# Large SBUF tiles on multiples of 512 bytes, and two query blocks in one visit of the attention

## The chip, the cores and the metric

One core of a Trainium2 chip runs the whole layer. The metric is the device time of one execution in microseconds (us); three runs of the kernel before gave 609.85, 610.11 and 610.28, median 610.11. Engines are called as in the profile: PE (matrix engine), PEld (its weight loads), DVE (vector), ACT (scalar), POOL (GpSimd), SP (sync, which issues most DMAs).

## The reference

The kernel computes one decoder layer for 512 tokens of width 1024 in float32. Cut to what matters:

```python
h = x @ w_in                                     # 1024 -> 9 x 1024
ua, va, za, qh, kh, vh, zb, ga, gb = split(h)
va = layer_norm(gelu(va)); sa = einsum(tril(w_s), va) + b_s
ya = gelu(ua) * sa * silu(za)
q, k = rope(qh) * 64 ** -0.5, rope(kh)           # 8 heads, two maps of 64 each
for each block of 128 queries:                   # causal
    sc = q_block @ k.T                           # two maps per head
    pr = softmax(where(kpos <= qpos, sc, -inf))
    o = (pr[map 0] - lam * pr[map 1]) @ v        # 128 values per head
yb = rms_norm(o) * 0.8 * silu(zb)
merged = sigmoid(ga) * (ya @ w_a) + sigmoid(gb) * (yb @ w_b)
ple = sigmoid(x @ w_pg) * (p @ w_ple)
out = layer_norm(2 ** 0.25 * x + merged @ w_out + ple)
```

## The kernel before

Every large product is done in three passes on numbers cut in two: a high part (rounded for the fast single-pass mode of PE) and a low part (the rest). `three` issues high x high, high x low and low x high, so a product costs three matmuls of 128 x 128 stationary by 512 moving columns; line 268, in `product`, issues all of them. The large products by token blocks use seven sub-products instead of eight (`quad`). The weights come as units of 128 x 1024 floats (512 KB) by DMA into `wr` tiles; ACT makes the high part (`wh`, line 389), DVE subtracts it (`wl`, line 392). Units are asked for, cut and used in a fixed rotation: `next_unit` works two to three units ahead.

The order of everything else is set by a clock that counts matmuls of the main stream: `product` adds one, and then runs what has come due in `agenda`, a heap of functions which `later(n, fn)` puts n matmuls ahead. All instructions are issued in that one order, and the engines' queues keep it (`manual_schedule`). So "23 later" below means 23 matmuls of the main stream.

The attention is woven into the stretch that projects keys, queries and ua (`rope`, `ua_pair`) and za. For each of 8 heads there are 4 blocks of 128 queries; block i has (i + 1) x 128 keys. `scores` (line 769) multiplies q with two forms of k into two `sc` banks (one per map); DVE adds the mask, scales and takes the minimum (line 776), then ACT takes the exponential with its row sum (line 782). `combine` weighs the two maps on DVE; `transposes` turns the result through PE with the identity `ident` into the one `tr` bank, which ACT copies out (line 805); `values` (line 814) multiplies by v into the head's `po` bank. `PERIOD` gives the distance of the blocks of a head in matmuls, 13, 16, 20 and 23 (72 per head; in the last two heads times 0.78), `COMBINE` when the maps are combined after the scores. The transposes of a block come with the scores of the block after next, the values with those of the one after that: at one point in the main stream PE does values of one block, transposes of another and scores of a third. This is called a visit here. After the last block, `squares`, `norm`, `scale`, `gated` and `turned` normalize the head and turn it (`TAIL`, `LAST_TAIL`).

The tiles of SBUF come from pools that are packed one after another: `consts`, `wraw`, `wsp`, `big` and `attn` (later `post`) from the left, `turning` (later `late`) from the right. Every tile is rounded to 32 bytes. `consts` holds the identity, some constants and rings of small tiles (`small`, one ring per tag).

Of the kernel before, what the change touches and what calls it, by code (L numbers as in the profile page):

```python
# [13 lines left out]
F32 = mybir.dt.float32  # L14
# [3 lines left out]
AF = mybir.ActivationFunctionType  # L18
# [3 lines left out]
P = 128  # L22
# [27 lines left out]
PERIOD = (13, 16, 20, 23)  # L50
COMBINE = (10, 11, 13, 12)
LAST_TURNS = (14, 27, 45)
PAIR = 144
TAIL = (2, 14, 26, 44, 56)
LAST_TAIL = (2, 10, 20, 32, 42)
# [178 lines left out]
def hybrid_layer(ctx: ExitStack, tc: tile.TileContext, a, out: bass.AP):  # L234
# [4 lines left out]
    consts = ctx.enter_context(tc.tile_pool(name="consts", bufs=1))  # L239
    wraw = ctx.enter_context(tc.tile_pool(name="wraw", bufs=1))  # L240
# [237 lines left out]
    ident = consts.tile([P, P], F32, name="ident")  # L478
# [10 lines left out]
    mhalf = consts.tile([P, 8], F32, name="mhalf")  # L489
# [17 lines left out]
    def small(shape, name, bufs=6):  # L507
        return consts.tile(shape, F32, name=name, tag=name, bufs=bufs)
# [254 lines left out]
    def scores(h, i):  # L763
        n = (i + 1) * P
        q, k0, k1 = stacks["q", h], stacks["k", h], stacks["kx", h]
        sc = [pbank("sc", 2) for _ in range(2)]
        for m in range(2):
            for o, kk in enumerate((k0, k1)):
                pe.matmul(sc[m][:, :n], q[:, m, i * P:(i + 1) * P], kk[:, m, :n],  # L769
                          start=o == 0, stop=o == 1)  # L770
        pr = [ap_.tile([P, T], F32, name=f"p{m}", tag=f"p{m}", bufs=3) for m in range(2)]
        if i == 0:
            todo["st", h] = small([P, NT, 4], "sth", 2)
        st = todo["st", h][:, i, :]
        for m in range(2):
            dve.tensor_tensor_reduce(out=pr[m][:, :n], in0=sc[m][:, :n], in1=mask[:, T - n:],  # L776
                                     scale=-(DK ** -0.5), scalar=3e38, op0=OP.add, op1=OP.min,
                                     accum_out=st[:, m:m + 1])
            if m == 0:
                dve.tensor_scalar(out=st[:, 0:1], in0=st[:, 0:1], scalar1=-math.log(T),  # L780
                                  scalar2=None, op0=OP.add)
            act.activation(pr[m][:, :n], pr[m][:, :n], AF.Exp, bias=st[:, m:m + 1], scale=-1.0,  # L782
                           accum_out=st[:, 2 + m:3 + m])
        todo[h, i] = pr, st

    def combine(h, i):
        n = (i + 1) * P
        pr, st = todo[h, i]
        r1 = small([P, 1], "r1")
        dve.reciprocal(out=r1, in_=st[:, 3:4])  # L790
        rho = small([P, 1], "rho")
        dve.tensor_scalar(out=rho, in0=r1, scalar1=st[:, 2:3], scalar2=neglam[:, 0:1],
                          op0=OP.mult, op1=OP.mult)
        dve.scalar_tensor_tensor(out=pr[0][:, :n], in0=pr[1][:, :n], scalar=rho[:, 0:1],
                                 in1=pr[0][:, :n], op0=OP.mult, op1=OP.add)
        todo[h, i] = pr[0]

    def transposes(h, i):
        n = (i + 1) * P
        ad = todo[h, i]  # L800
        tr = pbank("tr", 1)
        for j in range(i + 1):
            pe.transpose(tr[:, j * P:(j + 1) * P], ad[:, j * P:(j + 1) * P], ident)  # L803
        at = ap_.tile([P, T], F32, name="at", tag="at", bufs=2)
        act.activation(at[:, :n], tr[:, :n], AF.Copy)  # L805
        todo[h, i] = at

    def values(h, i):
        at = todo.pop((h, i))
        if i == 0:  # L810
            todo["po", h] = pbank("po", 1)
        po = todo["po", h]
        for j in range(i + 1):
            pe.matmul(po[:, i * P:(i + 1) * P], at[:, j * P:(j + 1) * P],  # L814
                      v[:, j, h * P:(h + 1) * P], start=j == 0, stop=j == i)

# [43 lines left out]
    def block(h, i, starts):  # L860
        e = NT * h + i
        later(starts[e], scores, h, i)
        later(starts[e] + COMBINE[i], combine, h, i)
        later(starts[e + 2], transposes, h, i)
        later(starts[e + 3], values, h, i)
        if i == NT - 1:
            tail = TAIL if h < 5 else LAST_TAIL
            for d, fn in zip(tail, (squares, norm, scale, gated)):
                later(starts[e + 3] + d, fn, h)

    def attention():
        starts = []
        for h in range(NH):
            stretch = 1.0 if h < NH - 2 else STRETCH
            at = PAIR * (h // 2) + BEGIN + h % 2 * sum(PERIOD) * stretch
            for n in PERIOD:
                starts.append(round(at))
                at += n * stretch
        starts += [starts[-1] + n for n in LAST_TURNS]
        for h in range(NH):  # L880
            for i in range(NT):
                block(h, i, starts)
        for h in range(NH - 1):
            later(starts[NT * h + 9], turned, h)
        later(starts[-1] + LAST_TAIL[4], turned, NH - 1)

# [214 lines left out]
    def rstd_of(st):  # L1101
        mv = small([P, 2], "mv")
        dve.bn_aggr(out=mv, in_=st)
        dve.tensor_scalar(out=mv[:, 1:2], in0=mv[:, 1:2], scalar1=EPS, scalar2=None, op0=OP.add)
        rs = small([P, 1], "rs")
# [343 lines left out]
```

## Time and profile before

| | us |
|---|---|
| median of 3 runs | 610.11 |
| profiled execution | 610.13 |
| its span (first to last instruction) | 608.2 |
| PE busy / DVE busy / ACT busy / POOL busy | 600.1 / 464.8 / 346.7 / 125.4 |
| idle of PE at the start, after the last matmul | 1.3, 6.7 |
| mean granted clock of PE over the span | 0.997 |

"Busy" counts the time in which at least one instruction of the engine runs. The matmuls are pipelined: one of 512 columns is shown some 0.39 us long, and the next starts before it ends, so the pace is read from starts, not from lengths. An instruction's row has its line, engine, operation, output and inputs by the names of the tiles, and the shape. In the groups, after the bar, stand busy us and mean ns, then the idle time before the group and what ended it.

### The profile page before, as it was taken

How to read it: one execution, taken by the hardware profiler on the slowest of the kernel's cores; microseconds unless marked ns; L12 is line 12 of the kernel's file. 1: busy time of each engine (PE TensorE's matmuls, PEld its weight loads, DVE VectorE, ACT ScalarE, POOL GpSimd, SP SyncE). 2: the span in 40 equal slices, each digit the busy share in tenths (PEclk: the TensorE clock that was granted, in tenths of full speed). 3: DMA queues.
4: the chain of work that ended last, by engine and by line, in shares of the span. 5: the costliest groups of instructions: out<-in, count | busy, mean ns of one | idle time of the engine just before them, and what ended most of it. 6: DMA issues, size and time to landing. Idle time of an engine off the chain costs nothing.

```text
span 608.2 us, 8270 instructions
## 1 busy us (share of the span) xinstructions
PE 600.1 (99%) x2880; PEld 503.1 (83%) x2880; DVE 464.8 (76%) x770; ACT 346.7 (57%) x537; POOL 125.4 (21%) x133
## 2 busy tenths in 40 slices
PE   9999999999999999999999999999999999999995
PEld 6888888888888888888888888888888888888885
DVE  6995645588789789678965788779687887879476
ACT  6656475755745745746676666554776565555310
POOL 1234121041252432422110321331120011110011
PEclk9999999999999999999999999999999999999998
DMA  8689899697887896892579988976999578997002
GB/s 309 228 246 182 252 205 227 237 240 252 277 208 277 273 258 230 240 313 61 150 310 288 305 241 217 273 175 191 286 244 306 172 206 250 253 256 288 27 35 103
DMA packets 44541, 138.23 MB, mean 227 GB/s; under 512 B 5940, under 2 KB 7092, under 8 KB 44148
## 3 DMA queue, kind: packets, MB, share of 16 engines
q1 hardware_dynamic: 34436, 102.97, 46.8%
q0 software_dynamic: 9488, 34.35, 30.6%
q8 instruction: 22, 0.36, 0.2%
q10 hardware_dynamic: 576, 0.39, 0.2%
q14 instruction: 19, 0.16, 0.1%
HBM read 118.69 MB, written 29.49 MB: 244 GB/s over the span
## 4 chain that ended last, share of the span: by engine, by line
PE 98%; DVE 1%; DMA 0%; DVEq 0%; issue 0%
PE ps_pp L268 56%; PE ps_sc L268 22%; PE ps_tx L268 9%; PE ps_sc L769 3%; PE ps_po L814 3%; PE ps_tr L803 1%; PE ps_po L268 1%; PE ps_tr L268 1%; PE ps_tr L1133 1%; PE ps_po L1133 1%; PE ps_tx L857 1%; DMA xr<-in_xT 0%; PE ps_po L1319 0%; PE ps_tr L1319 0%; DVE base L1361 0%; DVE xl L295 0%
## 5 line engine op out<-in xcount | busy, mean ns | idle before, releaser
L392 DVE TENSOR_TENSOR wl<-wr,wh 128x1024 fp32r<-128x1024 f32 x133 | 165.4, 1250 | 36.7 <-ACT wh L389 36.5
L389 ACT ACTIVATE wh<-wr 128x1024 fp32r<-128x1024 f32 x133 | 139.4, 1054 | 68.7 <-PE ps_pp L268 20.5
L268 PE MATMUL ps_pp<-xh,wh 128*128 128x512 f32 x232 | 91.2, 394 | 0.0
L268 PE MATMUL ps_pp<-xh,wl 128*128 128x512 f32 x232 | 91.0, 393 | 0.0
L268 PE MATMUL ps_pp<-xl,wh 128*128 128x512 f32 x232 | 90.4, 391 | 0.1
L365 POOL DMA_DIRECT2D wr<-in_w x30 | 25.8, 872 | 153.6 <-DVE wl L392 150.6
L268 PE MATMUL ps_pp<-wl,xh 128*128 128x512 f32 (+1 forms) x148 | 56.9, 384 | 0.0
L268 PE MATMUL ps_pp<-wh,xl 128*128 128x512 f32 (+1 forms) x148 | 56.8, 384 | 0.0
L268 PE MATMUL ps_pp<-wh,xh 128*128 128x512 f32 (+1 forms) x148 | 56.7, 383 | 0.0
L782 ACT ACTIVATE p<-p,sth 128x128 f32<-128x128 f32 (+3 forms) x64 | 35.5, 556 | 28.2 <-DVE sth L780 28.0
L268 PEld LDWEIGHTS ps_pp<-xl,wh 128*128 128x128 f32 x232 | 43.6, 188 | 9.3 <-DVE xl L295 0.5
L268 PEld LDWEIGHTS ps_pp<-xh,wh 128*128 128x128 f32 x232 | 43.5, 188 | 9.0 <-ACT wh L294 0.6
L268 PEld LDWEIGHTS ps_pp<-xh,wl 128*128 128x128 f32 x232 | 43.6, 188 | 8.7
L776 DVE CUSTOM_DVE_ANT_0 p<-ps_sc,mask 128x128 f32<-128x128 f32 (+3 forms) x64 | 31.0, 484 | 19.3 <-PE ps_sc L769 19.1
L268 PE MATMUL ps_sc<-wl,xsh 128*128 128x512 f32 x88 | 34.5, 392 | 0.0
L268 PE MATMUL ps_sc<-wh,xsh 128*128 128x512 f32 x88 | 34.4, 390 | 0.0
L268 PE MATMUL ps_sc<-wh,xsl 128*128 128x512 f32 x88 | 34.3, 390 | 0.0
L805 ACT ACTIVATE at<-ps_tr 128x128 f32<-128x128 f32 (+3 forms) x32 | 13.9, 436 | 32.9 <-PE ps_tr L803 27.5
L715 POOL TENSOR_TENSOR hl<-m,hl 128x512 fp32r<-128x512 f32 x16 | 23.4, 1502 | 43.9 <-ACT hl L710 26.6
L268 PEld LDWEIGHTS ps_pp<-wl,xh 128*128 128x128 f32 x148 | 27.8, 188 | 5.4
L268 PEld LDWEIGHTS ps_pp<-wh,xh 128*128 128x128 f32 x148 | 27.8, 188 | 5.4
L268 PEld LDWEIGHTS ps_pp<-wh,xl 128*128 128x128 f32 x148 | 27.8, 188 | 5.4
(304 smaller groups left out, 1335.2 us busy)
## 6 DMA issues: line engine op xcount, KB each, us to landing
wr<-in_w SPq DMA_DIRECT2D x83, 512.0 KB, 5.2
wr<-in_w POOLq DMA_DIRECT2D x30, 512.0 KB, 6.7
wa<-in_w POOLq DMA_DIRECT2D x12, 512.0 KB, 6.2
k<-hl SPq DMA_DIRECT2D x16, 256.0 KB, 4.8
q<-hl SPq DMA_DIRECT2D x16, 256.0 KB, 3.9
ws_va<-in_w POOLq DMA_DIRECT2D x8, 512.0 KB, 9.8
wr<-ws_va SPq DMA_DIRECT2D x8, 512.0 KB, 4.7
kx<-hl SPq DMA_DIRECT2D x12, 256.0 KB, 4.5
```

Of the source, the lines that this page charges most:

```text
L268: pe.matmul(ps, s, m, start=start, stop=stop, skip_group_check=read_within)
L365: pool.dma_start(out=raw[u], in_=weights(STEPS[FOLLOWS[u]][1]), accum_op=OP.add)
L389: act.activation(h, raw[u], AF.Copy)
L392: dve.tensor_tensor(out=l, in0=raw[u], in1=h.bitcast(F32), op=OP.subtract)
L715: pool.tensor_tensor(out=hl[:, 3 - j, :], in0=m[2 * j], in1=hl[:, j, :].bitcast(F32), op=OP.subtract)
L769: pe.matmul(sc[m][:, :n], q[:, m, i * P:(i + 1) * P], kk[:, m, :n], start=o == 0, stop=o == 1)
L776: dve.tensor_tensor_reduce(out=pr[m][:, :n], in0=sc[m][:, :n], in1=mask[:, T - n:], scale=-(DK ** -0.5), scalar=3e38, op0=OP.add, op1=OP.m ...
L782: act.activation(pr[m][:, :n], pr[m][:, :n], AF.Exp, bias=st[:, m:m + 1], scale=-1.0, accum_out=st[:, 2 + m:3 + m])
L803: pe.transpose(tr[:, j * P:(j + 1) * P], ad[:, j * P:(j + 1) * P], ident)
L805: act.activation(at[:, :n], tr[:, :n], AF.Copy)
L814: pe.matmul(po[:, i * P:(i + 1) * P], at[:, j * P:(j + 1) * P], v[:, j, h * P:(h + 1) * P], start=j == 0, stop=j == i)
L1133: pe.matmul(sa[:, t * P:(t + 1) * P], va[:, t, g * P:(g + 1) * P], aux[0][:, 0, g, :], start=True, stop=True)
```

## The change

Two things are changed.

First, the addresses. The identity moves from `consts` to a pool of its own (`edge`) at the right end of SBUF, in a tile of 248 columns of which 128 are used; `mhalf` grows from 8 to 80 columns; `mv` and `rs` take their tiles from the rings `r1` and `rho` that the attention has used. With that, `wr`, `wh`, `wl`, `xh`, `xl`, the tiles of the attention and those of the right side begin at multiples of 512 bytes. Before, those on the left began 96 bytes, those on the right 480 bytes past such a multiple. The free 384 bytes between the two sides are used up.

Second, the attention. Blocks 0 and 1 of a head become one group: in one `sc` bank per map block 0 has columns 0 to 127 and block 1 columns 128 to 383. Scores, combine, transposes (one copy out) and values of both are issued together, instruction for instruction as before. The periods become 24, 23 and 25 (72 again), the combine 15, 13 and 12, the tail shorter. The new `GROUPS` lists groups, blocks and columns.

PE, head 1 (values and transposes beside its first scores are still those of head 0). The numbers tell buffers apart, so equal numbers are one tile. `k` and `kx` are the two forms of the keys, `ps_sc` the two score banks, `ps_pp` a bank of the main stream. Before, the visit with the scores of block 0:

```order
L814 MATMUL ps_po_1219<-v_124,at_1224 128x128 x2
L803 MATMUL ps_tr_1290<-ident_98,p0_1167 128x128 x3
L769 MATMUL ps_sc_1296<-k_494,q_669 128x128
L769 MATMUL ps_sc_1296<-kx_1006,q_669 128x128
L769 MATMUL ps_sc_1297<-k_494,q_669 128x128
L769 MATMUL ps_sc_1297<-kx_1006,q_669 128x128
L268 MATMUL ps_pp_1181<-xh_91,wl_1053 128x512
```

and, 13 matmuls of the main stream later, that with the scores of block 1:

```order
L814 MATMUL ps_po_1219<-v_124,at_1294 128x128 x3
L803 MATMUL ps_tr_1341<-ident_98,p0_1232 128x128 x4
L769 MATMUL ps_sc_1348<-k_494,q_669 128x256
L769 MATMUL ps_sc_1348<-kx_1006,q_669 128x256
L769 MATMUL ps_sc_1349<-k_494,q_669 128x256
L769 MATMUL ps_sc_1349<-kx_1006,q_669 128x256
L268 MATMUL ps_pp_1328<-xh_91,wh_1109 128x512
```

Now one visit has the scores of both blocks:

```order
L820 MATMUL ps_po_1282<-v_127,at_1209 128x128 x3
L807 MATMUL ps_tr_1286<-ident_101,p0_1150 128x128 x3
L775 MATMUL ps_sc_1292<-k_497,q_672 128x128
L775 MATMUL ps_sc_1292<-kx_1009,q_672 128x128
L775 MATMUL ps_sc_1293<-k_497,q_672 128x128
L775 MATMUL ps_sc_1293<-kx_1009,q_672 128x128
L775 MATMUL ps_sc_1292<-k_497,q_672 128x256
L775 MATMUL ps_sc_1292<-kx_1009,q_672 128x256
L775 MATMUL ps_sc_1293<-k_497,q_672 128x256
L775 MATMUL ps_sc_1293<-kx_1009,q_672 128x256
L270 MATMUL ps_pp_1176<-xh_94,wl_1056 128x512
```

The eight score matmuls stand together; the values and transposes beside them are those of other groups. One visit of four per head is gone.

DVE, a later head: the rows that read the scores (`ISA` is the masked minimum, with its accumulator) and what stands behind them. Before, block 0 alone, with the subtraction for a weight unit (line 392) and the combine of block 0 (790, 792) behind it:

```order
L776 ISA p0_1540,sth_1542<-ps_sc_1534,mask_110 128x128
L776 ISA sth_1542 128x1
L780 TENSOR_SCALAR sth_1542<-sth_1542 128x1
L776 ISA p1_1541,sth_1542<-ps_sc_1535,mask_110 128x128
L776 ISA sth_1542 128x1
L392 TENSOR_TENSOR wl_1502<-wr2_1311,wh_1501 128x1024
L851 TENSOR_TENSOR on_1417<-on_1417,yb_754 128x512
L790 RECIPROCAL r1_1563<-sth_1542 128x1
L792 TENSOR_SCALAR rho_1565<-r1_1563,sth_1542,neglam_196 128x1
L794 SCALAR_TENSOR_TENSOR p0_1540<-p1_1541,rho_1565,p0_1540 128x128
```

Now, both blocks (the lines are shifted by 4):

```order
L780 ISA p0_1777,sth_1779<-ps_sc_1775,mask_113 128x128
L780 ISA sth_1779 128x1
L784 TENSOR_SCALAR sth_1779<-sth_1779 128x1
L780 ISA p1_1778,sth_1779<-ps_sc_1776,mask_113 128x128
L780 ISA sth_1779 128x1
L780 ISA p0_1777,sth_1779<-ps_sc_1775,mask_113 128x256
L780 ISA sth_1779 128x1
L784 TENSOR_SCALAR sth_1779<-sth_1779 128x1
L780 ISA p1_1778,sth_1779<-ps_sc_1776,mask_113 128x256
L780 ISA sth_1779 128x1
L394 TENSOR_TENSOR wl_1718<-wr2_1547,wh_1717 128x1024
```

Four reads of the score banks stand in one piece where there were two and two; line 394, the old 392, comes behind all of them.

The diff:

```diff
--- before.py
+++ after.py
@@ -47,12 +47,13 @@
 SWAP = 290
 BEGIN = 14
 STRETCH = 0.78
-PERIOD = (13, 16, 20, 23)
-COMBINE = (10, 11, 13, 12)
+GROUPS = (((0, slice(0, 128)), (1, slice(128, 384))), ((2, slice(0, 384)),), ((3, slice(0, 512)),))
+PERIOD = (24, 23, 25)
+COMBINE = (15, 13, 12)
 LAST_TURNS = (14, 27, 45)
 PAIR = 144
-TAIL = (2, 14, 26, 44, 56)
-LAST_TAIL = (2, 10, 20, 32, 42)
+TAIL = (2, 14, 24, 37)
+LATE_TAIL = (2, 10, 19, 29, 45)
 SILU = (122, 5)
 NORM = (174, 224, 276, 326)
 SPLITS = {'va': ((0, 10), (13, 16)), 'wb': ((4, 7), (13, 16)), '': ((0, 4), (6, 12))}
@@ -237,6 +238,7 @@
     ctx.enter_context(tc.manual_schedule())
 
     consts = ctx.enter_context(tc.tile_pool(name="consts", bufs=1))
+    edge = ctx.enter_context(tc.tile_pool(name="edge", bufs=1, side="right"))
     wraw = ctx.enter_context(tc.tile_pool(name="wraw", bufs=1))
     wsp = ctx.enter_context(tc.tile_pool(name="wsp", bufs=4))
     big = ctx.enter_context(tc.tile_pool(name="big", bufs=1))
@@ -475,7 +477,7 @@
 
     ask_xr(0)
 
-    ident = consts.tile([P, P], F32, name="ident")
+    ident = edge.tile([P, P + 120], F32, name="ident")[:, :P]
     make_identity(nc, ident)
 
     pool.memset(xr[:, 1, 0:1], 0.0)
@@ -486,7 +488,7 @@
     pool.memset(mask, 0.0)
     pool.affine_select(out=mask[:, T - P:], in_=mask[:, T - P:], compare_op=OP.is_ge, fill=-BIG,
                        base=0, pattern=[[-1, P]], channel_multiplier=1)
-    mhalf = consts.tile([P, 8], F32, name="mhalf")
+    mhalf = consts.tile([P, 80], F32, name="mhalf")
     pool.memset(mhalf, -0.5)
     halfpi = consts.tile([P, 1], F32, name="halfpi")
     pool.memset(halfpi, math.pi / 2)
@@ -760,60 +762,63 @@
 
     todo = {}
 
-    def scores(h, i):
-        n = (i + 1) * P
+    def scores(h, g):
         q, k0, k1 = stacks["q", h], stacks["k", h], stacks["kx", h]
         sc = [pbank("sc", 2) for _ in range(2)]
-        for m in range(2):
-            for o, kk in enumerate((k0, k1)):
-                pe.matmul(sc[m][:, :n], q[:, m, i * P:(i + 1) * P], kk[:, m, :n],
-                          start=o == 0, stop=o == 1)
         pr = [ap_.tile([P, T], F32, name=f"p{m}", tag=f"p{m}", bufs=3) for m in range(2)]
-        if i == 0:
+        if g == 0:
             todo["st", h] = small([P, NT, 4], "sth", 2)
-        st = todo["st", h][:, i, :]
-        for m in range(2):
-            dve.tensor_tensor_reduce(out=pr[m][:, :n], in0=sc[m][:, :n], in1=mask[:, T - n:],
-                                     scale=-(DK ** -0.5), scalar=3e38, op0=OP.add, op1=OP.min,
-                                     accum_out=st[:, m:m + 1])
-            if m == 0:
-                dve.tensor_scalar(out=st[:, 0:1], in0=st[:, 0:1], scalar1=-math.log(T),
-                                  scalar2=None, op0=OP.add)
-            act.activation(pr[m][:, :n], pr[m][:, :n], AF.Exp, bias=st[:, m:m + 1], scale=-1.0,
-                           accum_out=st[:, 2 + m:3 + m])
-        todo[h, i] = pr, st
-
-    def combine(h, i):
-        n = (i + 1) * P
-        pr, st = todo[h, i]
-        r1 = small([P, 1], "r1")
-        dve.reciprocal(out=r1, in_=st[:, 3:4])
-        rho = small([P, 1], "rho")
-        dve.tensor_scalar(out=rho, in0=r1, scalar1=st[:, 2:3], scalar2=neglam[:, 0:1],
-                          op0=OP.mult, op1=OP.mult)
-        dve.scalar_tensor_tensor(out=pr[0][:, :n], in0=pr[1][:, :n], scalar=rho[:, 0:1],
-                                 in1=pr[0][:, :n], op0=OP.mult, op1=OP.add)
-        todo[h, i] = pr[0]
-
-    def transposes(h, i):
-        n = (i + 1) * P
-        ad = todo[h, i]
+        todo[h, g] = pr
+        for i, cs in GROUPS[g]:
+            for m in range(2):
+                for o, kk in enumerate((k0, k1)):
+                    pe.matmul(sc[m][:, cs], q[:, m, i * P:(i + 1) * P], kk[:, m, :cs.stop - cs.start],
+                              start=o == 0, stop=o == 1)
+        for i, cs in GROUPS[g]:
+            st = todo["st", h][:, i, :]
+            for m in range(2):
+                dve.tensor_tensor_reduce(out=pr[m][:, cs], in0=sc[m][:, cs], in1=mask[:, T - (cs.stop - cs.start):],
+                                         scale=-(DK ** -0.5), scalar=3e38, op0=OP.add, op1=OP.min,
+                                         accum_out=st[:, m:m + 1])
+                if m == 0:
+                    dve.tensor_scalar(out=st[:, 0:1], in0=st[:, 0:1], scalar1=-math.log(T),
+                                      scalar2=None, op0=OP.add)
+                act.activation(pr[m][:, cs], pr[m][:, cs], AF.Exp, bias=st[:, m:m + 1], scale=-1.0,
+                               accum_out=st[:, 2 + m:3 + m])
+
+    def combine(h, g):
+        pr = todo[h, g]
+        for i, cs in GROUPS[g]:
+            st = todo["st", h][:, i, :]
+            r1 = small([P, 1], "r1")
+            dve.reciprocal(out=r1, in_=st[:, 3:4])
+            rho = small([P, 1], "rho")
+            dve.tensor_scalar(out=rho, in0=r1, scalar1=st[:, 2:3], scalar2=neglam[:, 0:1],
+                              op0=OP.mult, op1=OP.mult)
+            dve.scalar_tensor_tensor(out=pr[0][:, cs], in0=pr[1][:, cs], scalar=rho[:, 0:1],
+                                     in1=pr[0][:, cs], op0=OP.mult, op1=OP.add)
+        todo[h, g] = pr[0]
+
+    def transposes(h, g):
+        ad = todo[h, g]
         tr = pbank("tr", 1)
-        for j in range(i + 1):
-            pe.transpose(tr[:, j * P:(j + 1) * P], ad[:, j * P:(j + 1) * P], ident)
+        n = GROUPS[g][-1][1].stop
+        for c in range(0, n, P):
+            pe.transpose(tr[:, c:c + P], ad[:, c:c + P], ident)
         at = ap_.tile([P, T], F32, name="at", tag="at", bufs=2)
         act.activation(at[:, :n], tr[:, :n], AF.Copy)
-        todo[h, i] = at
-
-    def values(h, i):
-        at = todo.pop((h, i))
-        if i == 0:
+        todo[h, g] = at
+
+    def values(h, g):
+        at = todo.pop((h, g))
+        if g == 0:
             todo["po", h] = pbank("po", 1)
         po = todo["po", h]
-        for j in range(i + 1):
-            pe.matmul(po[:, i * P:(i + 1) * P], at[:, j * P:(j + 1) * P],
-                      v[:, j, h * P:(h + 1) * P], start=j == 0, stop=j == i)
-
+        for i, cs in GROUPS[g]:
+            for j in range(i + 1):
+                c = cs.start + j * P
+                pe.matmul(po[:, i * P:(i + 1) * P], at[:, c:c + P], v[:, j, h * P:(h + 1) * P],
+                          start=j == 0, stop=j == i)
 
     def squares(h):
         po = todo.pop(("po", h))
@@ -857,15 +862,14 @@
             pe.transpose(tr[:, i * P:(i + 1) * P], on[:, i, :], ident)
         act.activation(yb[:, h, :], tr, AF.Copy, scale=g08[:, 0:1])
 
-    def block(h, i, starts):
-        e = NT * h + i
-        later(starts[e], scores, h, i)
-        later(starts[e] + COMBINE[i], combine, h, i)
-        later(starts[e + 2], transposes, h, i)
-        later(starts[e + 3], values, h, i)
-        if i == NT - 1:
-            tail = TAIL if h < 5 else LAST_TAIL
-            for d, fn in zip(tail, (squares, norm, scale, gated)):
+    def group(h, g, starts):
+        e = len(GROUPS) * h + g
+        later(starts[e], scores, h, g)
+        later(starts[e] + COMBINE[g], combine, h, g)
+        later(starts[e + 2], transposes, h, g)
+        later(starts[e + 3], values, h, g)
+        if g == len(GROUPS) - 1:
+            for d, fn in zip(TAIL if h < 4 else LATE_TAIL, (squares, norm, scale, gated)):
                 later(starts[e + 3] + d, fn, h)
 
     def attention():
@@ -878,11 +882,11 @@
                 at += n * stretch
         starts += [starts[-1] + n for n in LAST_TURNS]
         for h in range(NH):
-            for i in range(NT):
-                block(h, i, starts)
+            for g in range(len(GROUPS)):
+                group(h, g, starts)
         for h in range(NH - 1):
-            later(starts[NT * h + 9], turned, h)
-        later(starts[-1] + LAST_TAIL[4], turned, NH - 1)
+            later(starts[3 * h + (7 if h < NH - 2 else 8)], turned, h)
+        later(starts[-1] + LATE_TAIL[4], turned, NH - 1)
 
     later(LAMBDAS[0], load_constants)
     for n, fn in zip(LAMBDAS[1:], (lam_dots, lam_exps, lam)):
@@ -1099,10 +1103,10 @@
     later(AUX[4], mask_ws)
 
     def rstd_of(st):
-        mv = small([P, 2], "mv")
+        mv = small([P, 2], "r1")
         dve.bn_aggr(out=mv, in_=st)
         dve.tensor_scalar(out=mv[:, 1:2], in0=mv[:, 1:2], scalar1=EPS, scalar2=None, op0=OP.add)
-        rs = small([P, 1], "rs")
+        rs = small([P, 1], "rho")
         pool.tensor_tensor(out=rs, in0=mv[:, 1:2], in1=mhalf[:, 0:1], op=OP.pow)
         return mv, rs
 
```

## The prediction

> **What bounds the kernel now.** I read the head of the profile's page first, then who waited for whom on the matrix engine, then its instructions one by one.
>
> ```profile
> span 608.2 us, 8270 instructions
> PE 600.1 (99%) x2880; PEld 503.1 (83%) x2880; DVE 464.8 (76%) x770; ACT 346.7 (57%) x537; POOL 125.4 (21%) x133
> PEclk9999999999999999999999999999999999999998
> PE 98%; DVE 1%; DMA 0%; DVEq 0%; issue 0%
> ```
>
> The chain of work that ended last is 98% PE, at full granted clock. A busy PE is not proof of a full PE, so the second view is the list of PE's waits. It has one row, the wait for the zeros of the warm-up:
>
> ```profile
> PE ps_po L462 <- DVE zeros L459: 1.3, 1, 1.3
> ```
>
> So PE never waits for data after the start. DVE, ACT, POOL and the DMA queues all run ahead of it, and a change in their work moves nothing until one of them falls behind. What is left is the pace of PE itself. The third view is the busy time of each engine by stretches (columns: us, PE, PEld, DVE, ACT, POOL with counts, granted clock, DMA share, GB/s), here one with nothing but 512-column matmuls and three that matter below:
>
> ```profile
> 20.00:110.00 90.00, 90.00 (x398) 74.51 (x397) 61.73 (x75) 53.75 (x69) 22.24 (x24) 1.00 0.86 219
> 110.00:310.00 200.00, 200.00 (x1057) 172.04 (x1056) 159.51 (x404) 120.73 (x253) 56.88 (x54) 1.00 0.76 230
> 310.00:388.00 78.00, 78.00 (x346) 64.59 (x345) 61.10 (x71) 51.07 (x66) 16.40 (x15) 1.00 0.94 284
> 424.00:440.00 16.00, 16.00 (x73) 13.23 (x72) 11.09 (x12) 11.48 (x15) 3.43 (x4) 1.00 1.02 284
> ```
>
> 398 matmuls touch 90 us, the first of them already running: 90/397 = 0.2267 us from start to start for 512 columns. The timeline of the end gives the pace for 256 columns, the first and the last of 24:
>
> ```profile
> 598.40 0.28 PE L268 MATMUL ps_pp<-wh,xh 128*128 128x256 f32 x1
> ...
> 601.16 0.28 PE L268 MATMUL ps_pp<-wh,xl 128*128 128x256 f32 x1
> ```
>
> 23 gaps in 2.76 us are 0.1200 us each. The two rows give a slope: 256 columns more cost 0.2267 - 0.1200 = 0.1067 us. So 512 columns are 0.2133 us of streaming, and each matmul, long or short, carries a constant 0.0133 us beside it. How many carry it (columns: PE and PEld busy with counts):
>
> ```profile
> 0.00:609.00 609.00, 546.93 (x2376) 440.10 (x2376) 1.00 0.78 227
> ```
>
> These are the matmuls of line 268; the scores on line 769 add 96 of 256 columns and more. So the constant adds up to 2472 x 0.0133 = 33 us. That is the only large thing here that is neither streaming nor done by another engine in PE's shadow, and it is what the first half of the change could touch.
>
> **The change part by part.** *Addresses.* In the program as built, the first raw-weight tile lies at byte 20,064 before, which is 39 x 512 + 96, and every large tile on the left side has the same 96 bytes over; those on the right side have 480. After, all of them have 0 (wr0 at 19,456, xh from 81,504 to 80,896, cs from 204,768 to 203,776). Only the phase moves. No instruction, size or order on any engine comes from it, and tiles on one side keep their places to each other. What can it cost or save? DMA rows of 4096 bytes per partition, DVE and ACT are in the shadow of PE, by the waits above. For PE's pace, the trace of before has no contrast: all moving operands of L268 and L769 start 96 bytes past a multiple of 128, so the 0.0133 us can be a fixed gap between two matmuls or a price of the offset. The bounds are therefore 0 and -33 us; a loss has no place to come from, since a tile that starts on a boundary touches no more memory lines than one that doesn't. I take 0. The constant is the same for 256 and 512 columns, which a fixed gap explains without any assumption; an offset explains it only if memory is read in lines of just the size (128 bytes, 32 columns) for which 96 bytes over costs one line more, and one line takes exactly 0.0133 us.
>
> The Trainium skill speaks against a gain too: "SBUF — State Buffer" (Specifications) gives SBUF lines of 16 bytes, and 96 and 480 are multiples of 16. By that rule the offset costs nothing and the sum stays as below; by the reading of one extra line it would be 33 us lower. No row here shows a line size.
>
> *Grouping.* Blocks 0 and 1 of a head share one visit: the same 8 score matmuls (4 x 128 and 4 x 256 columns), 3 transposes in one bank, one copy out, 3 value products. The number of matmuls stays at 2880 records. What goes are 8 interruptions of the main stream, one per head. What one costs beyond its own matmuls is read from two visits of head 1, blocks 0 and 1:
>
> ```profile
> 136.33 0.39 PE L268 MATMUL ps_pp<-xl,wh 128*128 128x512 f32 x1
> 136.56 0.60 PE L814 MATMUL ps_po<-v,at 128*128 128x128 f32 x4
> 137.00 0.49 PE L803 MATMUL ps_tr<-ident,p 128*128 128x128 f32 x3
> 137.24 0.31 PE L769 MATMUL ps_sc<-k,q 128*128 128x128 f32 x1
> 137.39 0.28 PE L769 MATMUL ps_sc<-kx,q 128*128 128x128 f32 x1
> ...
> 137.72 0.45 PE L268 MATMUL ps_pp<-xh,wl 128*128 128x512 f32 x1
> ...
> 138.70 0.39 PE L268 MATMUL ps_pp<-xh,wh 128*128 128x512 f32 x1
> ...
> 140.52 0.39 PE L268 MATMUL ps_pp<-xh,wl 128*128 128x512 f32 x1
> ...
> 143.49 0.39 PE L268 MATMUL ps_pp<-xh,wl 128*128 128x512 f32 x1
> ```
>
> From 136.33 to 138.70 are 2.37 us with five 512-column matmuls (1.133) and eleven of 128 columns; these run 0.109 apart (136.56 to 137.00 is four of them), so 1.199. That leaves 0.04 us. From 140.52 to 143.49 are 2.97 us with six of 512 (1.360), four of 256 (0.480) and ten of 128 (1.090): again 0.04. So eight visits less are 8 x 0.04 = **-0.3 us**. Between bounds: 0 if the longer visit pays the same again, -0.6 if both disappear.
>
> On the other engines the grouping removes 8 copies of the transposed maps on ACT and moves work. DVE and ACT by form, from the groups of 110 to 310 us:
>
> ```profile
> L776 DVE CUSTOM_DVE_ANT_0 p<-ps_sc,mask 128x256 f32<-128x256 f32 x16 | 6.7, 418 | 2.0 <-PE ps_sc L769 1.7
> L776 DVE CUSTOM_DVE_ANT_0 p<-ps_sc,mask 128x128 f32<-128x128 f32 x16 | 4.5, 284 | 9.0 <-PE ps_sc L769 9.0
> L776 DVE DVE_READ_ACCUMULATOR2_ANT sth<- 128x1 f32 x64 | 5.3, 83 | 0.0
> L780 DVE TENSOR_SCALAR sth<-sth 128x1 f32<-128x1 f32 x32 | 4.9, 154 | 1.1
> L805 ACT ACTIVATE at<-ps_tr 128x384 f32<-128x384 f32 x8 | 4.0, 494 | 6.5 <-PE ps_sc L769 5.4 <-PE ps_tr L803 1.2
> L805 ACT ACTIVATE at<-ps_tr 128x256 f32<-128x256 f32 x8 | 3.0, 375 | 2.2 <-PE ps_tr L803 2.2
> L805 ACT ACTIVATE at<-ps_tr 128x128 f32<-128x128 f32 x8 | 2.2, 278 | 19.4 <-PE ps_tr L803 19.4
> ```
>
> ACT saves 8 x (278 + 375 - 494) = 1.3 us, none of it on the path. DVE keeps its work but has it in one piece: 2 x 0.418 + 2 x 0.284 + 4 x 0.083 + 2 x 0.154 = 2.04 us per group, and its first instruction waits until PE has written the whole bank, some 0.5 us longer (four matmuls of 256 at 0.12). Behind it stand the subtraction that makes the low half of a weight unit (L392) and the rotations that empty PE's banks (L701). The weight unit is wanted two units of 24 matmuls later (11 us), the bank after at least one other group of 24 (5.4 us): covered. The visits now lie 23 to 25 matmuls apart instead of 13 to 23, so both score banks have longer to be read. The combine comes at most 15 matmuls after the scores, and the transposes 47 to 48 after them (29 to 43 before). No wait appears.
>
> *Small pieces.* The shared tags of mv and rs, and the larger mhalf, change where small tiles lie. The tail takes its new tiles from a ring of six, long after attention gave them back: 0.
>
> **The sum.** The profiled run took 610.13 us, its span is 608.2, and 1.9 lies around it. 610.1 + 0 (addresses) - 0.3 (grouping) = **609.8 us**. The median shown, 610.11, is the profiled run's time within 0.02, so no correction. I count 0.2% (1.2 us) as the least that can be told from no change; -0.3 is inside it. Own range of this case: 608.9 to 611.2, the -0.6 above with some scatter, and 1 us for a wait that I overlooked.
>
> **Rivals.** *The offset is what the 0.0133 us pays for.* For it: the constant fits one more line exactly, and both sides of memory were made to end on multiples at some expense of space. Against it: nothing in the trace varies with the address. Price: -33 us at most, 577. PE would then need its operands 5.9% faster. DVE (159.5 of 200 us) and ACT have room; the DMA has not where its share is 0.94 and 1.02 (310 to 388 and 424 to 440, 94 us), and there I count half of the 5.5 us as lost: about **580**. If only half of the constant goes, 593. The skill's "TensorE: Matmul & The Clock Gate" (Wait — 56ns, not 53.3ns?) has a fixed cost of about 2.5 ns per matmul of bf16; an estimate from that page leaves 2472 x 2.5 ns = 6 us of the 33, and the time is about 583. No row here shows that figure.
>
> *DVE falls behind at the group of two (slower).* It has a precedent in head 2, where DVE came to the scores late:
>
> ```profile
> 176.11 0.40 PE L769 MATMUL ps_sc<-kx,q 128*128 128x512 f32 x1
> ...
> 178.46 0.68 DVE L776 CUSTOM_DVE_ANT_0 p<-ps_sc,mask 128x512 f32<-128x512 f32 x1
> ...
> 179.26 0.68 DVE L776 CUSTOM_DVE_ANT_0 p<-ps_sc,mask 128x512 f32<-128x512 f32 x1
> ```
>
> The last read ended 3.8 us after the last score matmul had begun. With such a delay of 2.35 us, a group would end 2.35 + 2.04 = 4.4 us after it. The next visit comes 24 x 0.2267 = 5.4 us later, so it decides from a delay of 3.4 us; in the last two heads the period is multiplied by 0.78, 4.2 us, and PE would wait there. Per head I count 0.4 us of wait, 8 x 0.4 = 3.2, and **613**; the last two heads alone give 0.4, not to be told from nothing.
>
> *The padding does nothing for the address* (a tile is placed otherwise than written): excluded by the built program.
>
> **How the numbers follow.** No change but the grouping's 0.3: 0.55. Offset: 0.25 for the whole and 0.05 for a part. DVE behind: 0.13, and 0.02 for other losses. Predicted: 609.8. The range must reach the offset case, because without it about four in ten would be outside: 578 to 612.5; the likeliest case alone has 608.9 to 611.2. Faster is the two offset cases and a little of the first: 0.32; slower the last two: 0.15; same 0.53.
>
> **What would show it.** In the profile after, 512-column matmuls of L268's successor (now L270) should still start 0.2267 us apart in 20 to 110 us, and 256-column ones 0.1200. A pace of 0.213 to 0.220 refutes the first step and makes the offset the cause. PE's list of waits should still have only the warm-up; a row of scores or of ps_pp waiting for DVE in 110 to 310 us shows the DVE rival. There should be 28 visits with scores, transposes or values where 36 were (8 fewer), each with about 0.04 us beyond its matmuls, and the copy of the transposes (now L809) 24 times, 16 of 384 columns and 8 of 512.

## The result and the profile after

The median went from 610.27 us (609.72 to 611.05, 14 runs) to 611.11 (610.29 to 614.63, 14 runs): a ratio of 1.0015, 95% interval 1.0008 to 1.0022. The change makes the kernel 0.8 us slower where the forecast had 0.3 us less. That is small, and inside the range, but its sign is the other one. The profiled execution took 611.9 us.

The page of the profile after (head, clock, chain of waits):

```profile
span 610.2 us, 8250 instructions
PE 600.9 (98%) x2880; PEld 503.4 (82%) x2880; DVE 462.3 (76%) x770; ACT 344.6 (56%) x529; POOL 120.4 (20%) x133
PEclk9999999999999999999999999999999999999999
PE 82%; issue 8%; DMA 5%; DVE 2%; POOL 1%; ACT 0%; SPq 0%; DVEq 0%; ACTq 0%; POOLq 0%
```

The chain was 98% PE. Now 18% of it is not PE. That does not mean that 18% was lost: the chain, followed back from the end, meets a wait and goes on through what released it. Which wait, the list of PE's waits says:

```profile
PE ps_po L464 <- DVE zeros L461: 1.3, 1, 1.3
PE ps_sc L775 <- DMA q<-hl: 0.9, 1, 0.9
PE ps_sc L270 <- DVE wl L394: 0.3, 1, 0.3
```

Before there was the first row alone. The second is new: once, PE stands 0.9 us because queries have not landed. The third is not in every execution of the change: of four further profiles of kernels with the grouping, three (e2, e3, e5 below) don't have it and one (e6) does. None of the four without the grouping has it, so whether the change makes it more likely is not shown. The place of the second in PE's timeline of after:

```profile
250.92 0.30 PE L775 MATMUL ps_sc<-k,q 128*128 128x128 f32 x1
251.07 0.27 PE L775 MATMUL ps_sc<-kx,q 128*128 128x128 f32 x1
252.24 0.30 PE L775 MATMUL ps_sc<-k,q 128*128 128x128 f32 x1 [0.90 <-DMA q<-hl]
```

It is the first visit of head 6. Two matmuls of 128 columns should start 0.11 us apart; from 251.07 to 252.24 are 1.17, so 1.06 us are lost. The landing of the four loads of `q` issued in 236 to 256 us (heads 6 and 7; from issue to landing), before

```profile
DMA to landing us min/median/max: 2.4/3.3/4.1
```

and after:

```profile
DMA to landing us min/median/max: 2.6/7.3/7.8
```

Up to 3.7 us longer. Each head has two loads, one per map. PE waited for the second of head 6, so here are head 6's two alone (issued in 243.5 to 245.0 us), before

```profile
DMA to landing us min/median/max: 2.4/2.4/2.4
```

and after:

```profile
DMA to landing us min/median/max: 2.6/5.2/7.8
```

The first lands as before, the second 5.4 us later. The two (one row) are issued at nearly the same time in both kernels. SP and then POOL of before at that place (start, us, engine, operation):

```profile
244.02 1.18 SPq L731 DMA_DIRECT2D q<-hl  x2
```

```profile
241.13 2.86 POOL L715 TENSOR_TENSOR hl<-m,hl 128x512 fp32r<-128x512 f32 x2 [11.98 <-ACT hl L710]
244.51 1.95 POOL L840 TENSOR_TENSOR f<-ss,mhalf 128x4 f32<-128x4 f32 x1 [0.51 <-DVE ss L839]
246.82 1.04 POOL L847 TENSOR_TENSOR on<-on,f 128x512 f32<-128x512 f32 x1
247.80 1.75 POOL L324 DMA_DIRECT2D ws_pg<-in_w  x2
```

and of after:

```profile
243.67 1.19 SPq L733 DMA_DIRECT2D q<-hl  x2
```

```profile
241.11 2.53 POOL L717 TENSOR_TENSOR hl<-m,hl 128x512 fp32r<-128x512 f32 x2 [9.06 <-ACT hl L712]
243.58 0.87 POOL L326 DMA_DIRECT2D ws_pg<-in_w  x1
250.12 1.03 POOL L845 TENSOR_TENSOR f<-ss,mhalf 128x4 f32<-128x4 f32 x1 [5.68 <-DVE r L794]
...
252.50 0.89 POOL L326 DMA_DIRECT2D ws_pg<-in_w  x1
```

`ws_pg` is half of a weight sum that the kernel makes in DRAM: a DMA from POOL's queue that adds 512 KB of `in_w` to what lies there (`make_sums`, issued on line 324 before and 326 now). The norm of head 4 (`f`, `on`) stood ahead of it on POOL; after, the first of the two transfers is ahead of the norm. It is issued 4.2 us earlier, 0.09 us before the first loads of `q`, and runs beside them. The DMA queues in 243 to 249 us (q1 carries the loads that SP issues, q0 POOL's), before:

```profile
q1 hardware_dynamic: 498, 1.19, 58.1%
```

and after:

```profile
q0 software_dynamic: 107, 0.43, 50.8%
q1 hardware_dynamic: 147, 0.26, 14.5%
```

In six us SP's queue moves 0.26 MB where it moved 1.19; POOL's has half of all the engines' time. One packet of 4 KB of the adding transfer takes 0.508 x 16 x 6 us / 107 = 0.46 us.

How it comes to the swap is in the tables of the program, in matmuls of the main stream. `READY_MADE` asks for the `ws_pg` sums at 430 and 442, and neither kernel changes that. The last values of head 4 come three groups after its last scores, with the third of head 5, which is now 47 matmuls into that head instead of 29 (24 + 23 against 13 + 16): at 421, before at 403. The norm follows 10 later (`LATE_TAIL`, now used from head 4) instead of 14: at 431, before at 417. So 417 < 430 became 430 < 431.

### The profile page after: what moved, and what is told of

Same layout as the page of the kernel before. It is cut to its first block, busy times and chain, and to the rows that moved or that the text cites. A ratio compares the mean times of both kernels' runs of the same rounds, so it can differ in the third digit from the quotient of the medians.

```text
span 610.2 us, 8250 instructions
## 1 busy us (share of the span) xinstructions
PE 600.9 (98%) x2880; PEld 503.4 (82%) x2880; DVE 462.3 (76%) x770; ACT 344.6 (56%) x529; POOL 120.4 (20%) x133
## 4 chain that ended last, share of the span: by engine, by line
PE 82%; issue 8%; DMA 5%; DVE 2%; POOL 1%; ACT 0%; SPq 0%; DVEq 0%; ACTq 0%; POOLq 0%
PE ps_pp L270 47%; PE ps_sc L270 19%; PE ps_tx L270 6%; PE ps_sc L775 3%; DMA wr<-in_w 3%; PE ps_po L820 2%; DMA q<-hl 1%; PE ps_tr L807 1%; PE ps_po L270 1%; PE ps_tr L270 1%; POOL hl L717 1%; DVE wl L394 1%; PE ps_tr L1137 1%; PE ps_po L1137 1%; DMA wr<-ws_wb 1%
## 5 line engine op out<-in xcount | busy, mean ns | idle before, releaser
L809 ACT ACTIVATE at<-ps_tr 128x384 f32<-128x384 f32 (+1 forms) x24 | 12.7, 528 | 40.1 <-PE ps_tr L807 37.4
```

## The experiments

The theory after the result (A): the addresses do nothing, the grouping saves its 0.3 us, and the adding transfer that got ahead of the norm delays the loads of `q` and costs PE 1.1 us. Its rivals: the new addresses cost time; or the grouping itself costs it, by longer visits or a later tail, wherever the transfer stands (B).

**e1: the addresses alone.** The kernel before with the five edits on tiles (`ident` in `edge`, `mhalf` of 80, `mv` and `rs` in the rings `r1` and `rho`); the attention is as before.

```diff
+    edge = ctx.enter_context(tc.tile_pool(name="edge", bufs=1, side="right"))
-    ident = consts.tile([P, P], F32, name="ident")
+    ident = edge.tile([P, P + 120], F32, name="ident")[:, :P]
-    mhalf = consts.tile([P, 8], F32, name="mhalf")
+    mhalf = consts.tile([P, 80], F32, name="mhalf")
-        mv = small([P, 2], "mv")
+        mv = small([P, 2], "r1")
-        rs = small([P, 1], "rs")
+        rs = small([P, 1], "rho")
```

> The addresses alone, attention as before. Theory A (the addresses cost and save nothing; a transfer of the weights of pg that is issued too early costs the 0.8 us): within 0.3 us of before, 512-column matmuls 0.2267 us apart, no wait of PE for q. Rival B (the addresses themselves cost the 0.8 us, for instance at the start, where the first matmuls came 0.7 us later): 0.6 to 1.0 us slower than before, first scores of head 0 near 117.8 us instead of 117.05.

Measured: 610.32 us, ratio 0.9999 (0.9990 to 1.0007). PE waits for the warm-up alone, and the first scores of head 0 start at 117.16 us, so neither sign of rival B is there. Its busy time from 20 to 110 us:

```profile
20.00:110.00 90.00, 90.00 (x399) 74.53 (x398) 61.56 (x74) 53.22 (x68) 22.27 (x24) 1.00 0.85 220
```

399 matmuls touch the window where 398 did, one more or less at its edges; a pace without the 0.0133 us would have brought 422 (90/0.2133). Within the interval the addresses cost and save nothing.

**e2: the grouping alone.** The kernel after with these five edits undone.

```diff
-    edge = ctx.enter_context(tc.tile_pool(name="edge", bufs=1, side="right"))
-    ident = edge.tile([P, P + 120], F32, name="ident")[:, :P]
+    ident = consts.tile([P, P], F32, name="ident")
-    mhalf = consts.tile([P, 80], F32, name="mhalf")
+    mhalf = consts.tile([P, 8], F32, name="mhalf")
-        mv = small([P, 2], "r1")
+        mv = small([P, 2], "mv")
-        rs = small([P, 1], "rho")
+        rs = small([P, 1], "rs")
```

> The grouping alone, at the old addresses. Theory A: as the whole change, 0.6 to 1.0 us slower than before, with one wait of PE for q near 251 us of 0.5 to 1.1 us. Rival B: 0.3 us faster than before, since the grouping saves eight visits of 0.04 us.

Measured: 611.51 us, ratio 1.0015 (1.0006 to 1.0024), that of the whole change. PE's one wait after the warm-up:

```profile
PE ps_sc L774 <- DMA q<-hl: 0.9, 1, 0.9
```

The four loads of `q` land 7.1 us after their issue in the median, 7.9 at most. So the loss comes with the second half of the change, and the wait with it.

**e3: the transfer behind the norm again.** The kernel after with one number changed: the sums are asked for at 441, past norm (431) and scale (440) of head 4.

```diff
-'pg': (320, 430)
+'pg': (320, 441)
```

> The whole change, but the two accumulating transfers of the pg weights are due 11 matmuls later, so that on POOL they stand behind the norm and the scaling of head 4 again, as before the change. Theory A: the wait for q goes, 0.9 us less than the whole change, so 0.1 to 0.5 us faster than before. Rival B: stays 0.6 to 1.0 us slower than before. If q's wait goes and the time stays, the waits at 5, 307 and 529 us of the profile after are what cost.

Measured: 609.72 us, ratio 0.9989 (0.9980 to 0.9998). POOL issues the transfers in

```profile
251.68 1.74 POOL L326 DMA_DIRECT2D ws_pg<-in_w  x2
```

and `q` lands as before the change:

```profile
DMA to landing us min/median/max: 2.3/3.3/4.3
```

PE waits for the warm-up alone. In the same series e2 and e3 are 1.8 us apart. B would have left e3 slow. Theory A gave 0.1 to 0.5 us less than before; the medians are 0.8 apart, which is more, though the interval (0.1 to 1.2 us) takes those values in.

**e4: the transfer ahead of the norm, without the grouping.** The kernel before, its first sum asked for at 416, ahead of the norm of head 4 (417) and not at 430. The wider distance in the second line sets the second sum to 430; it was 442, and it stays behind the scale (429) on POOL. That line also moves the second copy, which starts the sum on SP, from 332 to 334. So "nothing else differs" is not quite so.

```diff
-'pg': (320, 430)
+'pg': (320, 416)
-                later(at[i] + APART * j, step, n, what, of, j)
+                later(at[i] + (APART + 2 * (name == "pg")) * j, step, n, what, of, j)
```

> The kernel before, with the first accumulating transfer of the pg weights due 14 matmuls earlier, so that on POOL it stands ahead of the norm of head 4, as in the change. Nothing else differs from before. Theory A: PE waits for q near 250 us, 0.5 to 1.1 us, and the kernel is 0.5 to 1.1 us slower than before. Rival B: no wait, within 0.2 us of before.

Measured: 612.24 us, ratio 1.0038 (1.0024 to 1.0052). PE's wait, and the landing of head 6's two loads:

```profile
250.66 0.28 PE L769 MATMUL ps_sc<-kx,q 128*128 128x128 f32 x1
253.00 0.30 PE L769 MATMUL ps_sc<-k,q 128*128 128x128 f32 x1 [2.07 <-DMA q<-hl]
```

```profile
DMA to landing us min/median/max: 2.7/5.4/8.2
```

The old attention gets the same kind of wait from the same swap, so the grouping is not needed for the loss. The wait is twice what was expected, 2.1 us against 0.9 in after, and the rows tell why. The load that PE waits for takes only 0.3 us longer than in after (8.2 against 7.8). But it is issued 0.44 us later (the two begin at 244.11, in after at 243.67), and PE is ready for it 0.41 us earlier (0.11 behind 250.66, in after behind 251.07). Together these make the 1.2 us. The second sum, issued here at 247.92 and in after at 252.50, can have a part in the 0.3 us at most; the loads of head 7, which land up to 14.4 us after their issue, are not waited for.

**e5: the transfer well ahead of the loads.** Is it harmful because it is ahead of the norm, or because it runs beside `q`? The kernel after, both sums asked for 36 matmuls earlier, ahead of the last rotation on POOL.

```diff
-'pg': (320, 430)
+'pg': (320, 394)
```

> The kernel after with its two accumulating transfers of ws_pg put 36 matmuls earlier, ahead of the rotation of the last queries on POOL's queue (some 8 us before the loads of q, beside those of k and kx). Theory A (the transfer costs time only because it shares the DMA engines with the loads of q for heads 6 and 7): these loads land in 4.5 us or less again, PE waits for nothing after the warm-up, median 609.4 to 610.2 (the -0.3 to -0.7 us of the experiment that put it behind). The loads of k and kx may take 1 to 5 us longer, but heads 6 and 7 use them 15 us later. Theory B (whatever comes ahead of head 4's norm on POOL or DVE delays the path, or the transfer is harmful wherever it stands): q late or another wait, 611 to 613.

Measured: 610.05 us, ratio 0.9993 (0.9984 to 1.0002). The transfers and `q`:

```profile
231.79 1.74 POOL L326 DMA_DIRECT2D ws_pg<-in_w  x2
```

```profile
DMA to landing us min/median/max: 2.4/3.3/4.2
```

No wait of PE after the warm-up, although the rotation on POOL, and with it the first loads of `q`, came 3.7 us later than in after:

```profile
247.32 1.18 SPq L733 DMA_DIRECT2D q<-hl  x2
```

The place ahead of the norm does no harm; being beside the loads of `q` does. This is A.

**e6: the same place, packets of 1 KB.** How does a transfer of 0.5 MB hold up loads on another queue? The kernel after, with the rows of these sums cut into four.

```diff
-accum_op=OP.add, max_dma_last_dim=4096)
+accum_op=OP.add, max_dma_last_dim=(1024 if name == 'pg' else 4096))
```

> The kernel after with the accumulating transfers of ws_pg cut into rows of 1024 bytes where they were 4096, at the same place. If the DMA engines take turns by packet, a load of q waits behind a quarter of the work at each turn and lands in 3.5 to 6 us: PE's wait of 0.9 us shrinks below 0.4, median 609.8 to 610.8. If the accumulation's whole work goes ahead of q, the landing stays at 7 us or grows (four times the packets), the wait stays at 0.9 us or more, median 611.2 to 613.

Measured: 609.83 us, ratio 0.9990 (0.9982 to 0.9998). The queues in 243 to 249 us and the landing of `q`:

```profile
q0 software_dynamic: 371, 0.38, 46.8%
q1 hardware_dynamic: 283, 0.52, 25.0%
```

```profile
DMA to landing us min/median/max: 2.4/6.2/6.8
```

A packet of the sum takes 0.468 x 16 x 6 / 371 = 0.12 us instead of 0.46, and SP's queue gets 283 packets through instead of 147. The four loads land 1 us earlier in the median (6.2 is a little above the expected 3.5 to 6). Of head 6's two the second, for which PE had waited, now lands 5.6 us after its issue and not 7.8:

```profile
DMA to landing us min/median/max: 2.4/4.0/5.6
```

That is near 249.8 us, and PE is ready for it at 251.18 as in after: the wait is gone with 1.4 us to spare. The Trainium skill's "DMA: Bandwidth & Descriptors" (Queues, rings and completion order) has each DMA engine go round its queues packet by packet. The counts agree in direction; they do not follow it in size, since a quarter of the packet's length gave SP's queue twice the packets and not four times. Whether the packets that the profile counts are the units by which the engines take turns, these runs do not tell.

**e7: e4 once more, for its clock.** The same program; what it is to settle stands in the last section.

> The kernel of e4_pg_ahead once more, for its profile alone: if the idle time of PE is what lowers the granted clock, the stretch 250 to 265 us shows again a wait of 1.5 to 2.5 us for q and behind it a granted clock below 0.95 in some slice of 5 us; if it was chance, the clock is 1.00 there although PE waits as long.

Measured: 612.44 us in one run, with a wait of 1.8 us and no fall of the clock: the fall in e4 does not come with every such wait.

## Why the prediction was wrong

*Addresses, 0 us: right.* The fixed 0.0133 us per matmul of 512 columns stays whether the tiles begin 96 and 480 bytes past a multiple of 512, as before, or at one, as in e1 and after (399 matmuls in 20 to 110 us in both). The prediction says that every matmul, long or short, carries this constant; its own 0.109 us for 128 columns is more than 0.0533 of streaming and 0.0133. Its sum counted 256 columns and more, so nothing came of it. So the rival of the offset (30% in all, down to 580 us) is out, and the low end of the range with it. The Trainium skill's "SBUF — State Buffer" (Specifications) gives lines of 16 bytes, of which 96 and 480 are multiples; that the offset costs nothing, as follows from it, agrees with e1.

*Grouping, 8 x 0.04 us less: right, term and size.* A visit with both blocks, in PE's timeline of e3:

```profile
136.06 0.39 PE L270 MATMUL ps_pp<-xl,wh 128*128 128x512 f32 x1
136.29 0.83 PE L820 MATMUL ps_po<-v,at 128*128 128x128 f32 x6
136.96 0.49 PE L807 MATMUL ps_tr<-ident,p 128*128 128x128 f32 x3
137.20 0.30 PE L775 MATMUL ps_sc<-k,q 128*128 128x128 f32 x1
...
138.08 0.28 PE L775 MATMUL ps_sc<-kx,q 128*128 128x256 f32 x1
138.20 0.40 PE L270 MATMUL ps_pp<-xh,wl 128*128 128x512 f32 x1
138.44 0.39 PE L270 MATMUL ps_pp<-xh,wh 128*128 128x512 f32 x1
```

From 136.06 to 138.44 are 2.38 us with two matmuls of 512 columns (0.453), 6 + 3 + 4 of 128 (1.417) and four of 256 (0.480): 0.03 are left, no more than in the shorter visits. Over the whole attention I added up, from the starts of all matmuls between 55 and 305 us, what lies beyond each one's pace (0.2267, 0.174, 0.1200 and 0.109 us by size):

| kernel | beyond the pace, us |
|---|---|
| before, e1 | 1.54, 1.54 |
| after, e2 | 2.28, 2.35 |
| e3, e5, e6 | 1.18, 1.18, 1.18 |

Without the wait the grouping saves 1.54 - 1.18 = 0.36 us. With it, after has 2.28, 1.10 more, which is the wait and what comes with it.

*DVE, ACT: right.* The copies of the transposes and the first read of a pair of score banks, groups of after in 110 to 310 us:

```profile
L809 ACT ACTIVATE at<-ps_tr 128x384 f32<-128x384 f32 x16 | 7.9, 493 | 24.9 <-PE ps_tr L807 22.3 <-DVE ss L840 2.6
L809 ACT ACTIVATE at<-ps_tr 128x512 f32<-128x512 f32 x8 | 4.8, 598 | 15.2 <-PE ps_tr L807 15.2
L780 DVE CUSTOM_DVE_ANT_0 p<-ps_sc,mask 128x128 f32<-128x128 f32 x16 | 4.6, 285 | 10.5 <-PE ps_sc L775 10.5
```

24 copies, 16 and 8, as forecast; DVE waits for PE's scores there, PE never for DVE. The rival "DVE falls behind" did not come.

*"No wait appears": this step failed.* It was argued for the engines on which the visits moved work, DVE, ACT and PE's banks. Of POOL and the DMA queues the prediction says only that they "run ahead" of PE; by how much, load by load, it does not ask, and the DMA issues on POOL's queue it does not go through. The tail of a head got "0" among the small pieces, for its tiles alone. But the norm of head 4 shifts from 417 to 431, 18 matmuls later by the new distances of the groups and 4 earlier by the shorter tail. (The distances were not followed to their end: the prediction has 47 to 48 matmuls from scores to transposes, the third group has 49.) The shift costs nothing on PE by itself; it changes POOL's queue, where the norm had been holding back a DMA. Before, that DMA was issued at 247.80 because the norm and scale of head 4 (244.51 to 247.86) stood ahead of it, and by then the loads of head 6 were home: the second is issued near 244.6 (the two take 1.18 us from 244.02) and lands 2.4 us later, at 247.1. PE wants it at 250.69:

```profile
250.69 0.28 PE L769 MATMUL ps_sc<-k,q 128*128 128x128 f32 x1
```

So this load had a margin of 3.6 us. In after it is issued 0.35 us earlier and wanted 0.5 later (251.18), which makes 4.5; its landing became 5.4 us longer, and the difference is the wait of 0.9. The margin stood in the trace of before, and the tables showed the swap. What sharing the DMA engines costs, the 5.4 us, is known from after alone.

The prediction's own range of this case (608.9 to 611.2) kept 1 us for "a wait that I overlooked", and the measured time lies in it. But no term of the sum stood for such a wait, and of the chances 0.02.

*The sum, put right.* Of the profiled execution after: -0.36 (visits), +1.06 (wait for `q`), +0.23 (the last head's transposes, in the same timeline of PE: the chain norm, scale, gated of `LATE_TAIL` ends too late for them, a tail that the prediction put at 0):

```profile
307.47 0.39 PE L270 MATMUL ps_pp<-xh,wl 128*128 128x512 f32 x1
307.93 0.63 PE L862 MATMUL ps_tr<-ident,on 128*128 128x128 f32 x4
```

0.46 us where 0.2267 is the pace. All five profiles with the grouping have this gap, none without. Together +0.9; measured +0.84 between the medians. The two profiled spans differ by 2.0, because after's execution lost another 0.75 us in its first 50 us and had the wait for a weight half. The first is not the change's: by the same count e3, whose first 50 us are the same program as after's, has 1.96 there, before 2.00 and after 2.74. It goes with the start of the clock. The warm-up's matmuls of 512 columns start 0.43 us apart, nearly twice the later 0.2267, and the clock records of the traces give the full clock from 4.36 us on in before, 4.83 in e3, 6.48 in after. The moment differs between executions of one program: 4.71 in e4 and 6.02 in e7. For e3 the sum gives -0.36 + 0.23 = -0.13; its median is 0.77 below, with an interval of 0.1 to 1.2, and e5 and e6, with the same sum, are 0.4 and 0.65 below. Whether they gain another 0.3 to 0.6 us that no trace shows stays open.

e3, the change with one number moved, is narrowly faster than the kernel before, and clearly faster than the change: 609.72 us against 610.49 and, for the grouping without it, e2's 611.51.

## What to carry to other kernels

Where one clock orders several in-order queues, a table of delays is an edit of every queue that its functions write to: list, for each moved function, the DMA issues that it passes on SP and POOL, and what else is landing then. A load whose landing was never waited for still has a margin, use minus landing, and that number (here 3.6 us before, 4.5 after) is what the delay by a moved transfer (here 5.4) is to be compared with. Take it for the one load that is used first: the median of all four hid both numbers. If a bulk transfer must run beside loads with a deadline, shorter packets can let them through, as in e6.

## What the hardware showed

An adding DMA from DRAM to DRAM on POOL's queue slows the loads of SP's queue far more than its bytes suggest: 0.43 MB of it in 6 us kept the other queue to 0.26 MB, where that had moved 1.19 without it. By the queues' rows its packets take 0.11 us per KB (0.508 x 16 x 6 us for 0.43 MB), SP's before 0.05 (0.581 x 16 x 6 for 1.19 MB). Cut to 1 KB they still take 0.12 us per KB: the shorter packets made the transfer no cheaper, they only let the loads in between. Whether the adding makes the packets long, or DRAM at both ends, or POOL's queue, was not tried; no run has a plain copy in that place.

In the profiled execution of e4 the granted clock of PE fell after the wait of 2.1 us (windows; the clock stands third from the right):

```profile
250.00:255.00 5.00, 2.93 (x17) 2.44 (x17) 2.01 (x7) 4.03 (x9) 0.00 (x0) 0.89 1.06 295
255.00:260.00 5.00, 5.00 (x28) 4.40 (x27) 2.10 (x9) 1.21 (x4) 0.00 (x0) 0.77 0.99 263
```

In e7, the same program on another occasion, PE waited 1.8 us at the same matmul, and the clock stayed:

```profile
250.00:255.00 5.00, 3.23 (x21) 2.79 (x20) 2.04 (x7) 4.21 (x9) 0.00 (x0) 1.00 1.06 299
255.00:260.00 5.00, 5.00 (x33) 4.47 (x32) 3.00 (x12) 2.85 (x8) 0.00 (x0) 1.00 1.00 263
```

28 matmuls instead of 33 touch the second stretch with the lower clock; 0.89 and 0.77 are half the clock for 1.1 and 2.3 us, and e4's clock records have it so, for 3.41 us from 253.88 on. Its profiled execution took 613.82 us, its median is 612.24, e7 took 612.44. Of the other four runs of e4, one (613.34) has as low a mean clock over the span (0.994, the profiled one 0.995), and so has one of the 14 of after (614.63, 0.993); no run of the kernels without this wait is below 0.996. A wait of 2 us can be followed by a lower clock and need not be; what decides it these runs do not tell.
